# A pair search on VectorE: decoding the selected pairs on a grid, with GpSimd's weight splits held back

## The chip, the cores and the metric

The kernel is one program on one core of a Trainium2 chip. The metric is device time in microseconds (us) of one execution, as a median of several runs. A core has five engines with a queue of their own each: TensorE (PE in the rows, PEld for its weight loads), VectorE (DVE), ScalarE (ACT), GpSimd (POOL) and SyncE (SP), which here only issues transfers. An engine works its queue in order; engines wait for each other by semaphores.

## The reference, cut to what matters

Two transformer blocks on 512 tokens of width 1024. The change lies in the expert layer (PEER) of the first block, between a mixing layer and a second block that it does not touch:

```python
q = (hf @ w_query).reshape(t, 8, 256)            # 8 heads
s1 = einsum('thd,hnd->thn', q[..., :128], keys1) # 128 keys each
s2 = einsum('thd,hnd->thn', q[..., 128:], keys2)
v1, i1 = top_k(s1, 16);  v2, i2 = top_k(s2, 16)
cand = (v1[..., :, None] + v2[..., None, :]).reshape(t, 8, 256)
sc, ci = top_k(cand, 16)                         # the 16 best pairs
e1 = take_along_axis(i1, ci // 16);  e2 = take_along_axis(i2, ci % 16)
idx = e1 * 128 + e2                              # one of 16384 experts
gates = softmax(sc)
a = gelu(einsum('td,thkd->thk', h, peer_u[idx]))
out = einsum('thk,thkd->td', gates * a, peer_v[idx])
```

So for each token and head the kernel must know, for 16 pairs, the two key numbers e1 and e2 and the pair's score.

## The kernel before, in words

All of it is in `peer`. Tokens lie on the 128 partitions, in four tiles of 128. Three tiles (384 tokens) are computed densely: every expert's `gelu(h . u)` for all of them, times a gate matrix that is zero where an expert was not selected, times `peer_v`. The fourth tile gathers its selected rows one by one with indirect transfers.

**Key search.** `head(h)` multiplies by one chunk of `w_query` (two tiles of 24 matmuls with 512 columns each), then by the keys (`ps_s`), and ScalarE copies the scores out (`s`). VectorE does the rest: `stage1` finds the 16 best of 128 for each half (MAX8, MATCH_REPLACE8 and FIND_INDEX8, 20 instructions for each half over four token tiles), `pairs` adds the 50 pair sums that can be among the 16 best (`cand`) while GpSimd adds the 50 expert numbers that go with them (`ce`), `stage2` finds the 16 best of 50, and `onehot` (once for each token tile) compares the 16 positions with 0 to 49 (`ob`), multiplies by `ce` (`oh`) and reduces, which gives the expert number (`Ef`).

**Weights.** Each fp32 weight tile is used as a rounded part `whi` (ScalarE) and a remainder `wlo = w - whi`. Line 94 computes `wlo`, in this part of the program on GpSimd (`eng=nc.gpsimd`). Of the three matmuls for one slice of weights the third reads `wlo`. Two raw tiles and four split tiles are buffered.

**Expert groups.** `u_group(g)` multiplies 256 experts' `peer_ut` by the 384 dense tokens: two tiles of 24 matmuls with 384 columns; ScalarE applies the gelu (`ga`). 64 groups are needed. Groups 0 to 9 run behind the eight heads, 10 to 15 in the gate stage, the other 48 in the value stage (`AHEAD = 32` tiles are computed before that).

**Gate stage.** `prep` turns the expert numbers and gates over (`ps_tr`). 96 calls of `g_build`, for four tokens each: VectorE compares with the two key numbers (`o1`, `o2`), GpSimd multiplies `o2` by the gate, TensorE multiplies the two (`ps_g`), ScalarE copies to `stg`; after eight calls 2 MB go to DRAM (`gd`). 

**Value stage.** For each tile of 128 experts the gates come back from DRAM (`gq`), multiply `ga`, and 18 matmuls add to six accumulators (`acc`); `u_group` is called every second tile, and the gathered rows are worked on beside it.

`todo` and `pull` say where the pieces of work are written; the framework's scheduler then sets the order within each engine's queue from what each piece needs, so written order is only a wish.

Of the kernel before, what the change touches and what calls it, by code (L numbers as in the profile page):

```python
# [8 lines left out]
F32 = mybir.dt.float32  # L9
F32R = mybir.dt.float32r  # L10
BF16 = mybir.dt.bfloat16
I32 = mybir.dt.int32
# [13 lines left out]
TT = T // P  # L26
AHEAD = 32
U1 = 10
# [23 lines left out]
class Kernel:  # L52
    def __init__(self, ctx, tc, io, tap=None):
        self.ctx, self.tc, self.nc, self.io = ctx, tc, tc.nc, io
        self.tap = tap or (lambda name, ap: None)
        self.sqtag = ("sq", "sqsum", 1, self.nc.vector)
        nc = self.nc
        self.const = ctx.enter_context(tc.tile_pool(name="const", bufs=1))
        self.res = ctx.enter_context(tc.tile_pool(name="res", bufs=1))
        self.wraw = ctx.enter_context(tc.tile_pool(name="wraw", bufs=2))  # L60
        self.wsp = ctx.enter_context(tc.tile_pool(name="wsp", bufs=4))
        self.act = ctx.enter_context(tc.tile_pool(name="act", bufs=1))
        self.tmp = ctx.enter_context(tc.tile_pool(name="tmp", bufs=2))
# [423 lines left out]
    def peer(self, x, r):  # L487
# [7 lines left out]
        nc.gpsimd.iota(it, pattern=[[1, P]], base=0, channel_multiplier=0, allow_small_or_imprecise_dtypes=True)  # L495
        Ef = c.tile([P, TT, 8, 16], F32, name="Ef")
        gt = c.tile([P, TT, 8, 16], F32, name="gt")
# [7 lines left out]
        with ExitStack() as st:  # L505
# [12 lines left out]
            with ExitStack() as s2:  # L518
                sp = s2.enter_context(tc.tile_pool(name="p_sel", bufs=2))
                pp = s2.enter_context(tc.tile_pool(name="p_ps", bufs=1, space=PSUM))  # L520
                it16 = sp.tile([P, 50, 16], BF16, bufs=1, name="it16")
                nc.vector.tensor_copy(it16, it[:, 0:50].unsqueeze(2).to_broadcast([P, 50, 16]))
                keys = sp.tile([P, 8, 2, P], F32, bufs=1, name="keys")
# [9 lines left out]
                def head(h):  # L533
# [29 lines left out]
                    box = {}  # L563

                    def pairs():
                        cand = sp.tile([P, TT, 50], F32, tag="cand", name="cand")
                        ce = sp.tile([P, TT, 50], F32, tag="ce", name="ce")
                        fi = sp.tile([P, 2, TT, 16], F32, tag="fi", name="fi")
                        nc.gpsimd.tensor_scalar(fi[:, 0], ix[:, :, 0, :], 128.0, None, op0=ALU.mult)
                        nc.gpsimd.tensor_copy(fi[:, 1], ix[:, :, 1, :])  # L570
                        o = 0
                        for i in range(8):
                            n = 16 // (i + 1)
                            nc.vector.tensor_tensor(cand[:, :, o:o + n], v[:, :, 0, i:i + 1].to_broadcast([P, TT, n]),
                                                    v[:, :, 1, 0:n], op=ALU.add)
                            nc.gpsimd.tensor_tensor(ce[:, :, o:o + n], fi[:, 0, :, i:i + 1].to_broadcast([P, TT, n]),
                                                    fi[:, 1, :, 0:n], op=ALU.add)
                            o += n
                        nc.vector.tensor_tensor(cand[:, :, o:50], v[:, :, 0, 8:16],
                                                v[:, :, 1, 0:1].to_broadcast([P, TT, 8]), op=ALU.add)  # L580
                        nc.gpsimd.tensor_tensor(ce[:, :, o:50], fi[:, 0, :, 8:16],
                                                fi[:, 1, :, 0:1].to_broadcast([P, TT, 8]), op=ALU.add)
                        box["cand"], box["ce"] = cand, ce

                    def stage2():
                        cand = box["cand"]
                        c2 = sp.tile([P, TT, 50], F32, tag="c2", name="c2")
                        sv = sp.tile([P, TT, 16], F32, tag="sv", name="sv")
# [10 lines left out]
                        for t in range(TT):  # L599
                            nc.vector.max_index(px[:, t, 8:16], sv[:, t, 8:16], c2[:, t, :])  # L600
                        pf = sp.tile([P, TT, 16], BF16, tag="pf", name="pf")
                        nc.vector.tensor_copy(pf, px)
                        box["pf"] = pf
# [3 lines left out]
                    def onehot(t):  # L607
                        ob = sp.tile([P, 50, 16], BF16, tag="ob", bufs=2, name="ob")
                        nc.vector.tensor_tensor(ob, it16, box["pf"][:, t, :].unsqueeze(1).to_broadcast([P, 50, 16]),
                                                op=ALU.is_equal)  # L610
                        oh = sp.tile([P, 16, 50], F32, tag="oh", bufs=2, name="oh")
                        nc.vector.tensor_tensor(oh, ob.rearrange("p c k -> p k c"),
                                                box["ce"][:, t, :].unsqueeze(1).to_broadcast([P, 16, 50]),
                                                op=ALU.mult)
                        nc.vector.tensor_reduce(Ef[:, t, h, :], oh, AX.X, ALU.add)

                    todo.extend([lambda: stage1(0), lambda: stage1(1), pairs, stage2] +
                                [lambda t=t: onehot(t) for t in range(TT)])

                for h in range(8):  # L620
                    head(h)
                    pull(4)
                for g in range(U1):
                    u_group(g, nc.gpsimd)
                    pull(3)
                pull(len(todo))
                g3 = gt.rearrange("p t h k -> p (t h) k")
# [8 lines left out]

            ah.append(st.enter_context(tc.tile_pool(name="p_ah1", bufs=AHEAD - 2 * U1)))
            Ei = c.tile([P, TT, P], I32, name="Ei")
            GQ = 32
            gd = st.enter_context(tc.tile_pool(name="p_dram", bufs=1, space=bass.MemoryType.DRAM)).tile(  # L640
                [NG // GQ, P, P, GQ], F32, name="gd")
            with ExitStack() as s3:
# [6 lines left out]
                def prep():  # L649
                    nc.vector.tensor_copy(Ei, Ef.rearrange("p t h k -> p t (h k)"))  # L650
                    scr = sp.tile([P, 3, 3, P], F32, tag="stg", name="scr")
                    e1, e1i, e2 = scr[:, 0], scr[:, 1].bitcast(I32), scr[:, 2]
                    nc.vector.tensor_scalar(e1i, Ei[:, 0:3, :], 7, None, op0=ALU.arith_shift_right)
                    nc.vector.tensor_copy(e1, e1i)
                    nc.vector.scalar_tensor_tensor(e2, e1, -128.0, Ef[:, 0:3].rearrange("p t h k -> p t (h k)"),
                                                   op0=ALU.mult, op1=ALU.add)
                    for i, src in enumerate((e1, e2, gt[:, 0:3].rearrange("p t h k -> p t (h k)"))):
                        ps = pp.tile([P, 4, P], F32, tag="g", name="ps_tr")
# [26 lines left out]
                for g in range(U1, AHEAD // 2):  # L685
                    pull(16)
                    u_group(g, nc.gpsimd)
                pull(len(todo))

            with ExitStack() as s4:  # L690
# [12 lines left out]
                def issue(n):  # L703
                    if n >= 2 * P:
# [6 lines left out]
                        out=rows[n], out_offset=None, in_=io[src],  # L711
                        in_offset=bass.IndirectOffsetOnAxis(ap=Ei[:, 3, j:j + 1], axis=0))
                    if len(done) > PACE:
# [685 lines left out]
```

## Time and profile before

| what | us |
|---|---|
| median of 3 runs | 3067.05 (3049.09, 3067.05, 3068.01) |
| profiled execution, its own time | 3052.26 |
| its span in the trace | 3050.5 |
| TensorE busy, of the span | 2882.1 (94%) |
| VectorE busy, of the span | 2066.8 (68%) |
| GpSimd busy, of the span | 768.9 (25%) |

The whole span is mostly TensorE's, so what counts is where TensorE is not busy. A view by stretches shows that; the chain of waits and the rows of single instructions say why. Matmul records overlap (a matmul of 512 columns shows 0.39 us, but the next starts 0.23 us later), so a stretch is costed by the distance between starts.

### The profile page before, as it was taken

What the parts mean: (1) busy time and instruction counts of PE and PEld (TensorE: products, weight loads), DVE (VectorE), ACT (ScalarE), POOL (GpSimd) and SP (SyncE); (2) the same over time, 40 slices, a digit from 0 to 9 for tenths busy, and PEclk for the clock granted to TensorE, in tenths of its full rate; (3) what the DMA queues carried; (4) which work ended last, traced back from release to release, by engine and by line L of the source; (5) the groups of instructions that cost most, each with busy time, mean ns of one, the idle gap of its engine ahead of it and who ended that gap; (6) DMA issues with size and microseconds to landing.
All of it is one profiled execution on the core that took longest, in us unless ns stands there. A gap on an engine that the chain in (4) does not pass through costs nothing. (4 is left out here: it accounts for less than half of the span.)

```text
span 3050.5 us, 39516 instructions
## 1 busy us (share of the span) xinstructions
PE 2882.1 (94%) x14965; PEld 2460.7 (81%) x14965; DVE 2066.8 (68%) x3945; ACT 1222.2 (40%) x2014; POOL 768.9 (25%) x646
## 2 busy tenths in 40 slices
PE   7989678879999999999998999999999999999998
PEld 5777677867999999989986777888887888878886
DVE  7979998767877787777876445444546776654453
ACT  6543125743333333333335435333335554443223
POOL 0013447743555554554431000000011010000000
PEclk9999798989999999999999999999999999999999
DMA  7541223578888888878862222222222011132221
GB/s 263 172 175 56 68 78 146 203 249 291 317 286 301 287 308 290 292 279 293 300 249 76 66 81 70 97 97 97 97 70 74 24 56 35 31 115 97 97 97 56
DMA packets 131937, 483.03 MB, mean 158 GB/s; under 512 B 10017, under 2 KB 59425, under 8 KB 95778
## 3 DMA queue, kind: packets, MB, share of 16 engines
q1 hardware_dynamic: 94016, 345.13, 32.4%
q0 software_dynamic: 36864, 134.23, 12.0%
q8 instruction: 118, 1.93, 0.3%
q10 hardware_dynamic: 866, 1.13, 0.1%
q14 instruction: 73, 0.60, 0.1%
HBM read 453.20 MB, written 27.26 MB: 158 GB/s over the span
## 5 line engine op out<-in xcount | busy, mean ns | idle before, releaser
L93 ACT ACTIVATE whi<-wraw 128x1024 fp32r<-128x1024 f32 (+2 forms) x500 | 522.5, 1046 | 1053.9 <-PE lin L122 708.2
L121 PE MATMUL lin<-xah,whi 128*128 128x512 f32 (+1 forms) x2144 | 798.4, 373 | 30.1 <-ACT ga L514 19.8
L123 PE MATMUL lin<-xah,wlo 128*128 128x512 f32 (+1 forms) x2144 | 794.2, 371 | 4.7 <-POOL wlo L94 4.7
L122 PE MATMUL lin<-xal,whi 128*128 128x512 f32 (+1 forms) x2144 | 794.2, 371 | 2.8 <-DVE xal L810 2.8
L94 DVE TENSOR_TENSOR wlo<-wraw,whi 128x1024 fp32r<-128x1024 f32 (+2 forms) x388 | 481.8, 1242 | 178.9 <-ACT whi L93 178.6
L94 POOL TENSOR_TENSOR wlo<-wraw,whi 128x1024 fp32r<-128x1024 f32 x112 | 298.3, 2673 | 779.1 <-ACT whi L93 682.6
L121 PEld LDWEIGHTS lin<-xah,whi 128*128 128x128 f32 x2144 | 407.1, 190 | 82.4 <-ACT ga L514 20.8
L122 PEld LDWEIGHTS lin<-xal,whi 128*128 128x128 f32 x2144 | 407.7, 190 | 49.5 <-DVE xal L810 5.1
L123 PEld LDWEIGHTS lin<-xah,wlo 128*128 128x128 f32 x2144 | 407.4, 190 | 49.3 <-POOL wlo L94 5.3
L721 DVE SCALAR_TENSOR_TENSOR gacc<-rows,acol,gacc 128x1024 f32<-128x1024 f32 x128 | 185.2, 1447 | 106.9 <-DMA rows<-peer_v,Ei 106.5
L769 PE MATMUL acc<-whi,gah 128*128 128x512 f32 x768 | 238.9, 392 | 19.5 <-ACT gah L93 19.5
L723 DVE CUSTOM_DVE_ANT_0 rows<-rows,hrow 128x1024 f32<-128x1024 f32 x128 | 191.1, 1493 | 96.9 <-DMA rows<-peer_u,Ei 96.7
L769 PE MATMUL acc<-whi,gal 128*128 128x512 f32 x768 | 239.5, 393 | 7.9 <-DVE gal L94 7.9
L769 PE MATMUL acc<-wlo,gah 128*128 128x512 f32 x768 | 238.1, 391 | 0.8 <-DVE wlo L94 0.8
L710 POOL DMA_INDIRECT rows<-peer_u,Ei x128 | 161.0, 1258 | 196.0 <-PE acc L769 143.0
L122 PE MATMUL lin<-hl,whi 128*128 128x512 f32 x512 | 200.1, 391 | 0.0
L121 PE MATMUL lin<-hh,whi 128*128 128x512 f32 x512 | 199.3, 389 | 0.0
L123 PE MATMUL lin<-hh,wlo 128*128 128x512 f32 x512 | 199.2, 389 | 0.0
L710 POOL DMA_INDIRECT rows<-peer_v,Ei x128 | 153.4, 1198 | 153.3 <-PE acc L769 112.0
L769 PEld LDWEIGHTS acc<-whi,gah 128*128 128x128 f32 x768 | 144.3, 189 | 47.1 <-ACT gah L93 19.8
L769 PEld LDWEIGHTS acc<-whi,gal 128*128 128x128 f32 x768 | 144.0, 189 | 41.7 <-DVE gal L94 11.6
L769 PEld LDWEIGHTS acc<-wlo,gah 128*128 128x128 f32 x768 | 144.7, 189 | 32.6 <-DVE wlo L94 1.4
(437 smaller groups left out, 4232.7 us busy)
## 6 DMA issues: line engine op xcount, KB each, us to landing
wraw<-peer_ut SPq DMA_DIRECT2D x64, 1024.0 KB, 5.2
wraw<-peer_v SPq DMA_DIRECT2D x64, 1024.0 KB, 6.3
wraw<-w_up SPq DMA_DIRECT2D x32, 1024.0 KB, 5.0
wraw<-w_down SPq DMA_DIRECT2D x32, 1024.0 KB, 5.0
gd<-stg SPq DMA_DIRECT2D x12, 2048.0 KB, 6.9
gq<-gd SPq DMA_DIRECT2D x32, 768.0 KB, 12.1
ada_w<-w_ada SPq DMA_DIRECT2D x20, 1024.0 KB, 5.2
wraw<-dn_w_in SPq DMA_DIRECT2D x16, 1024.0 KB, 5.1
```

What stands on the lines that cost most here:

```text
L93: self.nc.scalar.activation(hi, x, AF.Copy)
L94: (eng or self.nc.vector).tensor_tensor(lo, x, hi.bitcast(F32), op=ALU.subtract)
L121: nc.tensor.matmul(ps[:, :n], hi[:, i], xh[:, k, :n], start=(i == 0), stop=False)
L122: nc.tensor.matmul(ps[:, :n], hi[:, i], xl[:, k, :n], start=False, stop=False)
L123: nc.tensor.matmul(ps[:, :n], lo[:, i], xh[:, k, :n], start=False, stop=(k == ks[1] - 1))
L710: dma = nc.gpsimd.indirect_dma_start(out=rows[n], out_offset=None, in_=io[src], in_offset=bass.IndirectOffsetOnAxis(ap=Ei[:, 3, j:j + 1], ...
L721: nc.vector.scalar_tensor_tensor(gacc, t, w, gacc, op0=ALU.mult, op1=ALU.add)
L723: nc.vector.tensor_tensor_reduce(t, t, hrow, 1.0, 0.0, op0=ALU.mult, op1=ALU.add, accum_out=w)
L769: mm = nc.tensor.matmul(acc[t][d], w[:, ts], r[:, d * T:(d + 1) * T], start=(e == 0 and f == 0), stop=(e == P - 1 and f == 2))
```

## The change

Four parts.

1. **Grid and decoding.** The pair sums are laid out as a grid: 80 places in place of 50, written by three instructions in place of nine. The position in the grid gives row and column by shifts and comparisons; one comparison of 2048 bf16 elements with 0 to 15, one product with the key numbers and four halving sums then give e1 and e2 (bf16) for all four token tiles at once. GpSimd's `ce` is gone, and `prep` need no longer take expert numbers apart.
2. **Hold.** While head h (from 2 on) and group h-1 are split, each `wlo` on GpSimd also waits for head h-2's last decoding sum.
3. **Order.** Expert groups 0 to 6 are written between the heads. One group less (`AHEAD = 30`) runs before the value stage, which then has 49.
4. **Gate stage.** `o1` and `o2` have four buffers, not three; the twelfth gate write goes out in four pieces.

```diff
-AHEAD = 32
+AHEAD = 30
     def split(self, hi, lo, x, eng=None):
         self.nc.scalar.activation(hi, x, AF.Copy)
-        (eng or self.nc.vector).tensor_tensor(lo, x, hi.bitcast(F32), op=ALU.subtract)
+        ins = (eng or self.nc.vector).tensor_tensor(lo, x, hi.bitcast(F32), op=ALU.subtract)
+        if eng is not None and self.hold is not None:
+            self.after(ins, self.hold)
...
+                    C = 80
                     def pairs():
...
+                        nc.vector.tensor_tensor(cand[:, :, 16:72].rearrange("p t (i j) -> p t i j", j=8),
+                                                v0[:, :, 1:8].unsqueeze(3).to_broadcast([P, TT, 7, 8]),
+                                                v1[:, :, 0:8].unsqueeze(2).to_broadcast([P, TT, 7, 8]), op=ALU.add)
...
+                    def decode():
+                        px, sv = box["px"].bitcast(I32), box["sv"]
...
+                        nc.vector.tensor_scalar(rc[:, 0], px, 3, None, op0=ALU.arith_shift_right)
+                        nc.vector.tensor_scalar(rc[:, 1], px, 7, None, op0=ALU.bitwise_and)
...
+                        nc.vector.tensor_copy(ib, ix)
+                        oh = sp.tile([P, TT * 2 * 16, 16], BF16, tag="oh", bufs=1, name="oh")
+                        nc.vector.tensor_tensor(oh, it16, ij.rearrange("p t u k -> p (t u k)").unsqueeze(2)
+                                                .to_broadcast([P, P, 16]), op=ALU.is_equal)
+                        o4 = oh.rearrange("p (g k) i -> p g k i", k=16)
+                        nc.vector.tensor_tensor(o4, o4, ib.rearrange("p t u i -> p (t u) i").unsqueeze(2)
+                                                .to_broadcast([P, 2 * TT, 16, 16]), op=ALU.mult)
+                        for n in (8, 4, 2):
+                            nc.vector.tensor_tensor(oh[:, :, 0:n], oh[:, :, 0:n], oh[:, :, n:2 * n], op=ALU.add)
...
+                        return nc.vector.tensor_tensor(e, o5[:, :, :, 0], o5[:, :, :, 1], op=ALU.add)
...
+                last = []
                 for h in range(8):
-                    head(h)
-                    pull(4)
...
+                    self.hold = last[-2] if h > 1 else None
+                    last.append(head(h))
+                    if h:
+                        u_group(h - 1, nc.gpsimd)
+                self.hold = None
+                for g in range(7, U1):
                     u_group(g, nc.gpsimd)
...
-                    o1 = sp.tile([P, 4, P], F32, tag="o1", bufs=3, name="o1")
-                    o2 = sp.tile([P, 4, P], F32, tag="o2", bufs=3, name="o2")
+                    o1 = sp.tile([P, 4, P], F32, tag="o1", bufs=4, name="o1")
+                    o2 = sp.tile([P, 4, P], F32, tag="o2", bufs=4, name="o2")
...
-                        nc.sync.dma_start(out=gd[t0 // GQ], in_=box["stg"])
+                        cuts = (0, 8, 32, 64, P) if t0 + 4 == NG else (0, P)
+                        for a, b in zip(cuts, cuts[1:]):
+                            nc.sync.dma_start(out=gd[t0 // GQ][:, a:b, :], in_=box["stg"][:, a:b, :])
```

What this makes of three queues (line numbers of the changed kernel are 1 to 27 higher). GpSimd in the key search, before, at the first heads:

```order
L94 TENSOR_TENSOR wlo<-wraw,whi 128x1024 x2
L569 TENSOR_SCALAR fi<-ix 128x64
L94 TENSOR_TENSOR wlo<-wraw,whi 128x1024
L570 CAST fi<-ix 128x64
L576 TENSOR_TENSOR ce<-fi 128x4x16
L576 TENSOR_TENSOR ce<-fi 128x4x8
```

and with the change, from the first head to the gate stage (`o` is `o2`):

```order
L95 TENSOR_TENSOR wlo<-wraw,whi 128x1024 x4
L498 IOTA iota 128x128
L95 TENSOR_TENSOR wlo<-wraw,whi 128x1024 x36
L694 TENSOR_TENSOR o_3968<-o_3968,tr 128x512
```

The pair numbers are gone: GpSimd has nothing but splits until the gates begin. There, six single splits stand among the 96 products, where eight stood before.

VectorE at the end of head 0, before (one half of the four token tiles):

```order
L604 TENSOR_TENSOR gt<-sv 128x4x16
L602 CAST pf<-px 128x64
L609 TENSOR_TENSOR ob<-it_1871,pf 128x800 x2
L612 TENSOR_TENSOR oh<-ob,ce 128x800 x2
L615 TENSOR_REDUCE Ef<-oh 128x16 x2
```

and with the change (L555 is already head 1's first MAX8, L557 its MATCH_REPLACE8):

```order
L555 MAX v<-s 128x8
L620 TENSOR_TENSOR oh<-it_1871,ij 128x2048
L555 MAX v<-s 128x8
L623 TENSOR_TENSOR oh<-oh,ib 128x2048
L555 MAX v<-s 128x8
L626 TENSOR_TENSOR oh<-oh 128x128x8
L557 MATCH_REPLACE s_2161<-v,s 128x128
L626 TENSOR_TENSOR oh<-oh 128x128x4
L557 MATCH_REPLACE s_2161<-v,s 128x128
L626 TENSOR_TENSOR oh<-oh 128x128x2
L557 MATCH_REPLACE s_2161<-v,s 128x128
L631 TENSOR_TENSOR Ef<-oh 128x4x32
```

The next head's first searches now stand ahead of this head's last sum (L631), the one that GpSimd is held on two heads later.

ScalarE where the softmax's exponential stands, before (`ga` is an expert group's gelu):

```order
L514 ACTIVATE ga<-lin 128x384
L629 ACT_TABLE_LOAD
L629 ACTIVATE gt<-gt 128x512
L93 ACTIVATE whi<-wraw 128x1024
L514 ACT_TABLE_LOAD
L514 ACTIVATE ga<-lin 128x384
```

and with the change (`scr` are the copies of e1 and e2 in `prep`):

```order
L517 ACTIVATE ga<-lin 128x384
L650 ACT_TABLE_LOAD
L650 ACTIVATE gt<-gt 128x512
L517 ACT_TABLE_LOAD
L517 ACTIVATE ga<-lin 128x384
L94 ACTIVATE whi<-wraw 128x1024 x2
L517 ACTIVATE ga<-lin 128x384
L673 ACTIVATE scr<-Ef 128x384 x2
```

Ahead of the exponential stand the gelus of groups 0 to 6 now, and behind it those of 7, 8 and 9.

## Rows read from the trace of the kernel before

**Rows 1.** Windows: length, busy us per engine (instructions), granted clock, DMA share, GB/s.

```profile
236.00:481.00 245.00, 187.70 (x934) 170.35 (x933) 244.67 (x959) 61.95 (x87) 109.70 (x122) 0.88 0.22 74
481.00:642.00 161.00, 143.01 (x1065) 138.93 (x1063) 124.43 (x196) 116.87 (x123) 121.85 (x105) 0.98 0.46 185
...
775.00:1595.00 820.00, 817.56 (x4121) 741.63 (x4120) 631.54 (x688) 290.24 (x403) 406.55 (x267) 1.00 0.81 290
```

**Rows 2.** The same view, two stretches of 25 us inside the key search.

```profile
250.00:275.00 25.00, 25.00 (x127) 20.85 (x125) 24.96 (x97) 7.86 (x12) 7.33 (x14) 1.00 0.25 80
...
325.00:350.00 25.00, 15.17 (x63) 13.09 (x64) 25.00 (x111) 5.49 (x8) 9.98 (x14) 0.69 0.13 43
```

**Rows 3.** Timeline, VectorE, search: start, duration, work; last the final head.

```profile
235.85 0.87 DVE L552 MAX8 v<-s 128x8 f32<-128x128 f32 x4 [5.31 <-ACT s L547]
...
245.22 1.07 DVE L574 TENSOR_TENSOR cand<-v 128x64 f32<-128x64 f32 x8
...
246.42 0.55 DVE L591 MAX8 sv<-cand 128x8 f32<-128x50 f32 x4
...
249.50 0.82 DVE L604 TENSOR_TENSOR gt<-sv 128x64 f32<-128x64 f32 x1
...
263.49 0.87 DVE L552 MAX8 v<-s 128x8 f32<-128x128 f32 x4
...
460.68 0.62 DVE L604 TENSOR_TENSOR gt<-sv 128x64 f32<-128x64 f32 x1
...
473.92 1.90 DVE L615 TENSOR_REDUCE Ef<-oh 128x16 f32<-128x800 f32 x2
```

**Rows 4.** Durations by line, 225 to 480 us: shortest/median/longest, first and last start.

```profile
L609 DVE TENSOR_TENSOR ob<-it,pf x32: 550/564/2614, 250.5 to 470.1; 128x800 bf16<-128x800 bf16 x32
...
L612 DVE TENSOR_TENSOR oh<-ob,ce x32: 1573/1727/3865, 251.4 to 472.3; 128x800 f32<-128x800 bf16 x32
...
L602 DVE CAST pf<-px x8: 178/2360/2404, 250.2 to 461.2; 128x64 bf16<-128x64 uint32 x8
...
L94 POOL TENSOR_TENSOR wlo<-wraw,whi x35: 2340/2398/3966, 233.6 to 476.9; 128x1024 fp32r<-128x1024 f32 x35
```

**Rows 5.** The page: VectorE's full-precision subtract (busy us, mean ns of one).

```profile
L94 DVE TENSOR_TENSOR wlo<-wraw,whi 128x1024 fp32r<-128x1024 f32 (+2 forms) x388 | 481.8, 1242 | 178.9 <-ACT whi L93 178.6
```

**Rows 6.** Timeline, TensorE: scores of two heads, expert matmuls, stall, transposes.

```profile
246.75 1.05 PE L545 MATMUL ps_s<-keys,q 128*128 128x128 f32 x8
...
259.54 1.05 PE L545 MATMUL ps_s<-keys,q 128*128 128x128 f32 x8
...
440.77 0.33 PE L122 MATMUL lin<-xal,whi 128*128 128x384 f32 x1
...
449.61 0.33 PE L122 MATMUL lin<-xal,whi 128*128 128x384 f32 x1
...
464.77 0.69 PE L121 MATMUL lin<-xah,whi 128*128 128x384 f32 x1 [14.65 <-ACT ga L514]
...
480.76 1.10 PE L660 MATMUL ps_tr<-ident,scr 128*128 128x128 f32 x6 [0.79 <-PE lin L123]
```

**Rows 7.** Timeline of TensorE late in the gate stage; then its longest wait there.

```profile
624.93 1.05 PE L676 MATMUL ps_g<-o,o 128*128 128x128 f32 x8
...
632.89 1.05 PE L676 MATMUL ps_g<-o,o 128*128 128x128 f32 x8
...
PE ps_g L676 <- POOL o L674: 17.6, 10, 2.3
```

**Rows 8.** Timeline, TensorE, end of gate stage; then a DMA row (page).

```profile
638.60 1.16 PE L676 MATMUL ps_g<-o,o 128*128 128x128 f32 x8 [0.41 <-POOL o L674]
...
641.35 0.34 PE L123 MATMUL lin<-xah,wlo 128*128 128x384 f32 x1
661.15 1.22 PE L769 MATMUL acc<-whi,gah 128*128 128x512 f32 x2 [19.45 <-ACT gah L93]
...
gd<-stg SPq DMA_DIRECT2D x12, 2048.0 KB, 6.9
```

More of the change, by code (lines that the diff above doesn't have):

```diff
@@ L571, in pairs @@
[L571 to L583, printed above, removed]
+                        cand = sp.tile([P, TT, C], F32, tag="cand", name="cand")
@@ new lines, in pairs @@
+                        v0, v1 = v[:, :, 0, :], v[:, :, 1, :]
+                        nc.vector.tensor_tensor(cand[:, :, 16:72].rearrange("p t (i j) -> p t i j", j=8),
+                                                v0[:, :, 1:8].unsqueeze(3).to_broadcast([P, TT, 7, 8]),
+                                                v1[:, :, 0:8].unsqueeze(2).to_broadcast([P, TT, 7, 8]), op=ALU.add)
+                        nc.vector.tensor_tensor(cand[:, :, 0:16], v0[:, :, 0:1].to_broadcast([P, TT, 16]), v1,
+                                                op=ALU.add)
@@ L585, in stage2 @@
+                        nc.vector.tensor_tensor(cand[:, :, 72:80], v0[:, :, 8:16],
+                                                v1[:, :, 0:1].to_broadcast([P, TT, 8]), op=ALU.add)
+                        box["cand"] = cand
                     def stage2():
                         cand = box["cand"]
-                        c2 = sp.tile([P, TT, 50], F32, tag="c2", name="c2")
+                        c2 = sp.tile([P, TT, C], F32, tag="c2", bufs=1, name="c2")
                         sv = sp.tile([P, TT, 16], F32, tag="sv", name="sv")
@@ L600, in stage2 @@
                             nc.vector.max_index(px[:, t, 8:16], sv[:, t, 8:16], c2[:, t, :])
-                        pf = sp.tile([P, TT, 16], BF16, tag="pf", name="pf")
-                        nc.vector.tensor_copy(pf, px)
-                        box["pf"] = pf
+                        box["px"], box["sv"] = px, sv
+                    def decode():
+                        px, sv = box["px"].bitcast(I32), box["sv"]
+                        rc = sp.tile([P, 2, TT, 16], I32, tag="rc", name="rc")
+                        nc.vector.tensor_scalar(rc[:, 0], px, 3, None, op0=ALU.arith_shift_right)
+                        nc.vector.tensor_scalar(rc[:, 1], px, 7, None, op0=ALU.bitwise_and)
+                        rf = sp.tile([P, 2, TT, 16], F32, tag="rf", name="rf")
+                        nc.vector.tensor_copy(rf, rc)
+                        r, q = rf[:, 0], rf[:, 1]
+                        w = sp.tile([P, 3, TT, 16], F32, tag="w", name="w")
+                        ij = sp.tile([P, TT, 2, 16], BF16, tag="ij", name="ij")
+                        m, a, b = [w[:, i] for i in range(3)]
+                        nc.vector.scalar_tensor_tensor(m, r, 9.0, q, op0=ALU.is_equal, op1=ALU.mult)
+                        nc.vector.scalar_tensor_tensor(a, r, 1.0, r, op0=ALU.is_ge, op1=ALU.subtract)
+                        nc.vector.tensor_tensor(ij[:, :, 0, :], m, a, op=ALU.subtract)
+                        nc.vector.tensor_scalar(b, r, 1.0, 8.0, op0=ALU.is_equal, op1=ALU.mult)
+                        nc.vector.tensor_tensor(b, b, q, op=ALU.add)
+                        nc.vector.tensor_tensor(ij[:, :, 1, :], b, m, op=ALU.subtract)
+                        ib = sp.tile([P, TT, 2, 16], BF16, tag="ib", name="ib")
+                        nc.vector.tensor_copy(ib, ix)
[7 more added lines that the diff above has]
+                            nc.vector.tensor_tensor(oh[:, :, 0:n], oh[:, :, 0:n], oh[:, :, n:2 * n], op=ALU.add)
+                        e = Ef[:, :, h].rearrange("p t u k -> p t (u k)")
+                        o5 = oh.rearrange("p (t g) i -> p t g i", t=TT)
@@ L617, in head @@
-                    todo.extend([lambda: stage1(0), lambda: stage1(1), pairs, stage2] +
-                                [lambda t=t: onehot(t) for t in range(TT)])
-                for h in range(8):
-                    head(h)
-                    pull(4)
-                for g in range(U1):
+                        return nc.vector.tensor_tensor(e, o5[:, :, :, 0], o5[:, :, :, 1], op=ALU.add)
+                    stage1(0)
+                    stage1(1)
+                    pairs()
+                    stage2()
@@ L624, in peer @@
+                    return decode()
+                last = []
+                for h in range(8):
+                    self.hold = last[-2] if h > 1 else None
+                    last.append(head(h))
+                    if h:
+                        u_group(h - 1, nc.gpsimd)
+                self.hold = None
+                for g in range(7, U1):
                     u_group(g, nc.gpsimd)
-                    pull(3)
-                pull(len(todo))
                 g3 = gt.rearrange("p t h k -> p (t h) k")
@@ L649, in prep @@
                 def prep():
-                    nc.vector.tensor_copy(Ei, Ef.rearrange("p t h k -> p t (h k)"))
                     scr = sp.tile([P, 3, 3, P], F32, tag="stg", name="scr")
[L652 to L657, printed above, removed]
+                    for i in range(2):
+                        nc.scalar.activation(scr[:, i].rearrange("p t (h k) -> p t h k", k=16), Ef[:, 0:3, :, i, :],
+                                             AF.Copy)
+                    nc.vector.scalar_tensor_tensor(Ei.rearrange("p (h k) -> p h k", k=16), Ef[:, 3, :, 0, :], 128.0,
+                                                   Ef[:, 3, :, 1, :], op0=ALU.mult, op1=ALU.add)
+                    for i, src in enumerate((scr[:, 0], scr[:, 1], gt[:, 0:3].rearrange("p t h k -> p t (h k)"))):
                         ps = pp.tile([P, 4, P], F32, tag="g", name="ps_tr")
```

30 lines of the change are left out of this document (9 added, 21 removed).

## The prediction, made before the changed kernel ran

> **What bounds the kernel now.** I read the view by stretches first, to see where TensorE, 94% busy over the whole span, is not. From 775 us on it is full: 817.56 of 820 us at clock 1.00 [rows 1], so nothing is to be had there, and what is moved there is paid in full. In the key search it is busy 187.70 of 245 us, and VectorE 244.67 [rows 1]: that stretch is VectorE's. In the gate stage TensorE is busy 143.01 of 161 us, and VectorE, ScalarE and GpSimd 117 to 124 each [rows 1]: four engines in lock step, none full. The clock follows: with TensorE busy 25.00 of 25 us it was granted 1.00 (2.4 GHz), with 15.17 of 25 us 0.69, a mixture with 1.2 GHz [rows 2].
>
> Next the timeline of VectorE, from the search's first MAX8 at 235.85 to its last reduce, which ends at 475.82 [rows 3]: 240.0 us for 8 heads, **30.0 us a head**. In head 0 the two searches of 128 take 9.37 us (to 245.22), the pair sums 1.20, the search of 50 takes 3.08 (to 249.50), and the other 14 us go to `gt`, `pf` and `onehot`.
>
> Then durations by line. `pf`, a cast of 64 elements, takes 178 ns at best and 2360 at the median; `ob` 550 at best and 2614 at worst; `oh` 1573 and 3865 [rows 4]. The excess is always near 2.1 to 2.3 us, and a split `wlo` on GpSimd lasts 2398 ns [rows 4]: these instructions wait for one to end.
>
> **The change, part by part.** *VectorE's work for a head.* The searches stay: 9.37. Three grid sums in place of nine: 0.7. The search of 80 lies between that of 50 (3.08) and half the searches of 128 (9.37/2 = 4.69, as many instructions): 3.08 + 30/78 x 1.61 = 3.7. `gt` 0.2. Ten small instructions of decoding at the 178 ns of `pf` alone: 1.8. The comparison of 2048 bf16 elements has no row. At `ob`'s best rate (550 ns for 800) it is 1.4 us; at the 1242 ns for 1024 of a full-precision subtract [rows 5] 2.5; at `oh`'s strided rate (1573 for 800) 4.0. I take 2.4: like `ob` its operands are bf16, but one of them repeats a single element 16 times, so I don't count on `ob`'s rate. The product, 2048 in contiguous runs, at `ob`'s rate: 1.4. Three halving sums of 1024, 512 and 256: 0.7, 0.4 and 0.25. The last sum reads 128 elements with a stride, as `oh` does: 0.3. Together **21.2 us** (20.2 to 23.5).
>
> *The hold.* Once head h-2's last sum is in, GpSimd splits four tiles, 4 x 2.4 = 9.6 us; meanwhile VectorE searches head h-1, which takes 9.37 us and reads one tensor an instruction. So the splits should be over when the decoding, which suffers from them, comes. They end about when the grid sums begin; for a part of one split there I add 0.7: 21.9 us.
>
> The Trainium skill, page SBUF — State Buffer, section Who interferes with whom, speaks against the change: a VectorE instruction with two SBUF inputs and a GpSimd instruction that reads SBUF exclude each other for a whole instruction, and the decoding has many two-input instructions. The excess in `ob` and `oh` agrees [rows 4]. By the page alone, with splits and decoding falling together as before, nothing would be won here; the hold is what decides, and rival 2 is that case.
>
> *TensorE's cycle.* From one head's scores to the next 12.79 us pass [rows 6]: projection and scores. A group adds 48 matmuls at 8.84/51 = 0.1733 us [rows 6], 8.32. Together 21.1 us, just under VectorE's 21.9. A cycle c of 21.9 with TensorE near full should keep the full clock.
>
> *Does the hold delay it?* From release: split 2.4, projection 48 matmuls 10.9, copies and scores 2.5, then the rest of the previous head's decoding, which stands behind the new head's first MAX8 on VectorE, 2.3. That is 18.1 us, within 21.9: no wait.
>
> *End of the search.* Head 0 ends at 235.85 + 21.2 = 257.1, head 6 at 257.1 + 6c. Head 7's `gt` follows 13.2 later (searches, less four MAX8 already done, grid, search of 80). The exponential on ScalarE waits for it, and groups 8 and 9 on TensorE wait behind: the same wait shows before as 14.65 us up to 464.77, 3.5 us after `gt` (460.68 + 0.62) [rows 3, 6]. Groups 8 and 9 then take 16.6, and 2.2 for the clock after the stall. So the transposes start at 293 + 6c = **425** where they started at 480.76 [rows 6]: **-56 us**. With c at TensorE's 21.1 it is 420 (-61); with one whole split more in each head, c = 23.6, it is 435 (-46).
>
> *Gate stage.* Six builds took 7.96 us with 15 group matmuls among them [rows 7]: 5.36 without, 0.894 for a build. Before: 96 builds 85.8, 288 matmuls 49.9, transposes 1.2, together 136.9; it took 160.8 (480.76 to 641.5). So 23.9 us were lost, the largest wait TensorE's on GpSimd's product, 17.6 us in 10 waits [rows 7]; eight splits stood among the products, 3.0 us for each. Now one group less runs here (-8.3, which leaves 128.6), six splits stand there, and the fourth buffer lets VectorE run one build (1.3 us) further ahead: 6 x 1.7 = 10 us lost. That makes 139, **-22 us** (-32 if nothing is lost, -14 if the buffer does nothing).
>
> *Value stage.* The group that moved costs 8.3 us where TensorE is full: **+8.3**.
>
> *The last gate write.* TensorE stood still for 19.45 us from the last gates to the first value matmul [rows 8]. Before, 11 group matmuls (2 us) filled its start; now none is left, +2. The write takes 6.9 us [rows 8]; in pieces the first gates are in DRAM earlier, but `gq` stands behind all four pieces on SyncE's queue and reads the same rows of DRAM: at most 6 us gained, at least nothing. I take 1, so **+1** (-4 to +2). The other edits (a wider table of 0 to 15, ScalarE's copies in `prep`) lie in waits: VectorE idles 5.31 us ahead of the first MAX8 [rows 3].
>
> **Sum:** -56 - 22 + 8.3 + 1 = -69 on the profiled execution's 3052.3: 2984. It stands 14.8 below the median of the runs (3049 to 3068); I add half of that: **2990**.
>
> **The rivals.** *1. The gate stage stays in lock step* (18%): the splits cost what they did and the buffer nothing, so that only the moved group leaves: -8.3 in place of -22, about 3005. For it: GpSimd's products and splits alone are 121.85 us of the stage's 161 [rows 1], and ScalarE's copies 117.
>
> *2. The hold doesn't part splits and decoding* (7%). Four splits in 22 us can catch more two-input instructions than before; if a head stays near 30 us, the search ends at 473, 8 us earlier, and the total is 3052 - 8 - 22 + 9 + 7 = 3038: no difference. Against it: the splits need 9.6 us and the searches give 9.4 free of them.
>
> *3. The hold starves TensorE and the clock falls* (5%, slower). If the release of a split comes late, TensorE idles in each cycle, is granted 1.2 GHz as at 325 us [rows 2], and its 21.1 us become 42. The search then ends at 293 + 253 = 546, 65 later: 3052 + 65 - 13 + 7 = 3111. It decides from c = 33: there the gains behind the search are used up. Against it: 21.1 of 21.9 us is as full as the stretch with clock 1.00.
>
> **How the numbers follow.** The forecast has 70%. Its bounds are -61 - 32 + 8.3 - 4 = -89, and -46 - 14 + 8.3 + 2 = -50 with the median's full 14.8 added: 2963 to 3017. Rival 1 falls in it; rivals 2 and 3 lie outside. The range is 2960 to 3018. What a measurement can tell from no change is 1%, here 31 us: faster means under 3036. The forecast, rival 1 and a little of rival 2 make 90% faster; the rest of rival 2 is 5% same; rival 3 is 5% slower.
>
> **What would show it.** VectorE's MAX8 of successive heads 21 to 23 us apart, and the comparison near 2.4 us; the product at most 1.5 us with no long outliers in heads 1 to 5; the clock at 1.00 all through the search; the transposes near 425; 139 us from there to the last gates; about 19 to 21 us of stillness behind it. Heads 25 us or more apart would make the prediction wrong, and so would a clock under 0.9 there, or a value stage longer by more than one group.

## The result and the profile after

Median 3009.38 us (3007.77 to 3015.08, 4 runs) against 3065.31 (3049.09 to 3068.01, 4 runs): ratio **0.9834** [0.9814, 0.9853], faster by 1.7%. Forecast were 2990, range 2960 to 3018. The profiled execution took 3015.08 us, its span 3013.4.

The medians are 56 us apart, the two profiled executions 37: the one before (3052.26) lies low among its kernel's times, the one after is the longest of its four. The stretches below compare these two executions; in which stretch the other 19 us lie no trace here shows.

Three stretches first. The view of the changed kernel's stretches gives their bounds, then the length, busy time and count of TensorE, its weight loads, VectorE, ScalarE and GpSimd, then granted clock, DMA share and GB/s. The bounds are 236 us as in [rows 1] (the first MAX8 stands at 237.16), the transposes, the last build's end; and the value matmuls from first to last. Behind them, the last two stretches of the kernel before.

```profile
236.00:429.01 193.01, 179.58 (x940) 162.49 (x939) 179.29 (x932) 63.48 (x90) 83.21 (x35) 0.96 0.27 93
429.01:583.74 154.73, 140.15 (x1018) 137.54 (x1016) 124.14 (x195) 113.98 (x120) 116.20 (x103) 0.93 0.44 178
608.64:1564.36 955.72, 941.85 (x4656) 843.56 (x4656) 726.96 (x818) 331.55 (x459) 452.71 (x301) 1.00 0.80 286
...
480.76:639.76 159.00, 141.32 (x1055) 137.56 (x1056) 124.67 (x196) 115.60 (x122) 121.85 (x105) 0.98 0.46 186
661.15:1601.16 940.01, 931.32 (x4608) 834.29 (x4608) 720.91 (x818) 328.67 (x455) 445.80 (x299) 1.00 0.81 290
```

The transposes start at 429.0 where they started at 480.8 [rows 6]: **-51.8**. From there to the first value matmul 179.6 us pass, 180.4 before (480.76 to 661.15 [rows 6, 8]): **-0.8**. The value stage takes 955.7 us for 4656 matmuls; the kernel before took 940.0 for 4608: **+15.7**. Together -36.9, and the spans differ by 37.1.

In the middle of the search TensorE is full now, where [rows 2] show 15.17 us of 25 at clock 0.69; over the whole search the clock is 0.96.

```profile
325.00:350.00 25.00, 24.95 (x133) 22.41 (x132) 24.69 (x143) 8.49 (x12) 13.06 (x6) 1.00 0.24 85
```

VectorE's decoding in the search, all heads together; columns are minimum, median and maximum in ns, first and last start in us.

```profile
L626 DVE TENSOR_TENSOR oh<-oh x24: 408/452/2941, 256.5 to 417.2; 128x1024 bf16<-128x1024 bf16 x8, 128x512 bf16<-128x512 bf16 x8, 128x256 bf16<-128x256 bf16 x8
L620 DVE TENSOR_TENSOR oh<-it,ij x8: 2274/2292/2293, 252.8 to 407.9; 128x2048 bf16<-128x2048 bf16 x8
L623 DVE TENSOR_TENSOR oh<-oh,ib x8: 1204/1226/2800, 255.2 to 410.7; 128x2048 bf16<-128x2048 bf16 x8
L631 DVE TENSOR_TENSOR Ef<-oh x8: 399/426/448, 258.6 to 417.7; 128x128 bf16<-128x128 bf16 x8
```

The comparison (L620) takes 2.29 us in every head, the product 1.23 at the median. Compare the medians with the maxima: a split still falls into the decoding now and then. The timeline of VectorE and GpSimd shows where it doesn't (head 3 to head 4) and where it does (head 6); columns are start, duration, engine, line.

```profile
323.31 0.44 DVE L631 TENSOR_TENSOR Ef<-oh 128x128 bf16<-128x128 bf16 x1
323.99 9.49 POOL L95 TENSOR_TENSOR wlo<-wraw,whi 128x1024 fp32r<-128x1024 f32 x4 [11.93 <-DVE v L555]
333.03 0.70 DVE L573 TENSOR_TENSOR cand<-v 128x224 f32<-128x224 f32 x1
...
381.76 2.37 POOL L95 TENSOR_TENSOR wlo<-wraw,whi 128x1024 fp32r<-128x1024 f32 x1 [1.51 <-ACT whi L94]
381.79 2.42 DVE L615 TENSOR_TENSOR w<-w,rf 128x64 f32<-128x64 f32 x1
...
388.08 2.41 POOL L95 TENSOR_TENSOR wlo<-wraw,whi 128x1024 fp32r<-128x1024 f32 x1 [3.95 <-ACT whi L94]
388.09 3.91 DVE L626 TENSOR_TENSOR oh<-oh 128x1024 bf16<-128x1024 bf16 x3
```

Four splits run right behind the last sum, while VectorE searches, and end as the grid sums begin. The splits of groups 7 to 9 have no hold in the program, and two of them fall into head 6's decoding: an add of 64 elements takes 2.42 us beside a split of 2.37. Last sums of successive heads are 21.4 to 21.8 us apart up to head 5 and 25.9 and 25.7 in heads 6 and 7.

TensorE's timeline at the end of the search; the bracket is its idle time ahead and what ended it.

```profile
408.83 0.69 PE L124 MATMUL lin<-xah,whi 128*128 128x384 f32 x1 [9.32 <-ACT ga L517]
420.55 0.44 PE L124 MATMUL lin<-xah,whi 128*128 128x384 f32 x1 [1.21 <-ACT ga L517]
429.01 0.82 PE L680 MATMUL ps_tr<-ident,scr 128*128 128x128 f32 x6
```

This answers to the 14.65 us of [rows 6]. The gate stage, GpSimd's splits and TensorE's waits there:

```profile
439.39 2.37 POOL L95 TENSOR_TENSOR wlo<-wraw,whi 128x1024 fp32r<-128x1024 f32 x1 [1.19 <-ACT whi L94]
...
442.81 1.29 PE L696 MATMUL ps_g<-o,o 128*128 128x128 f32 x8 [2.32 <-POOL o L694]
...
456.83 2.37 POOL L95 TENSOR_TENSOR wlo<-wraw,whi 128x1024 fp32r<-128x1024 f32 x1 [2.19 <-ACT whi L94]
...
460.25 1.64 PE L696 MATMUL ps_g<-o,o 128*128 128x128 f32 x8 [2.29 <-POOL o L694]
...
477.52 1.82 PE L696 MATMUL ps_g<-o,o 128*128 128x128 f32 x8 [2.29 <-POOL o L694]
```

Six splits stand among the products, some 17.3 us apart. GpSimd waits for ScalarE's copy (1.19 us at the first split, 2.2 at the others) and splits for 2.37, and TensorE stands for 2.3; the eight matmuls behind take 1.29, then 1.64, then 1.82. The stage's clock is 0.93; before it was 0.98. Behind the gates:

```profile
593.25 1.08 SPq L777 DMA_DIRECT2D gq<-gd  x2
594.38 3.19 SPq L101 DMA_DIRECT2D wraw<-peer_v  x1
607.35 1.49 DVE L784 TENSOR_TENSOR ga<-ga,gq 128x384 f32<-128x384 f32 x3
608.64 1.22 PE L793 MATMUL acc<-whi,gah 128*128 128x512 f32 x2 [24.90 <-ACT gah L94]
```

TensorE stands for 24.90 us where it stood 19.45 [rows 8]: `gq` is issued 9.5 us behind the last gates and used 14.1 us later; before, 8.4 and 11.8.

### The profile page after: what moved, and what is told of

Read it like the earlier page. It is cut to its first block, busy times and chain, and to the rows that moved or that the text cites. A ratio compares the mean times of both kernels' runs of the same rounds, so it can differ in the third digit from the quotient of the medians.

```text
span 3013.4 us, 39409 instructions
## 1 busy us (share of the span) xinstructions
PE 2883.6 (96%) x14965; PEld 2462.2 (82%) x14965; DVE 2011.0 (67%) x3918; ACT 1223.4 (41%) x2016; POOL 740.5 (25%) x558
## 5 line engine op out<-in xcount | busy, mean ns | idle before, releaser
L95 DVE TENSOR_TENSOR wlo<-wraw,whi 128x1024 fp32r<-128x1024 f32 (+2 forms) x388 | 488.2, 1260 | 175.9 <-ACT whi L94 175.7
L95 POOL TENSOR_TENSOR wlo<-wraw,whi 128x1024 fp32r<-128x1024 f32 x112 | 291.3, 2615 | 855.4 <-ACT whi L94 682.9
L793 PE MATMUL acc<-whi,gah 128*128 128x512 f32 x768 | 238.4, 392 | 24.9 <-ACT gah L94 24.9
L734 POOL DMA_INDIRECT rows<-peer_v,Ei x128 | 159.8, 1249 | 162.6 <-PE acc L793 127.3
```

Of the source, the lines that this page charges most:

```text
L95: ins = (eng or self.nc.vector).tensor_tensor(lo, x, hi.bitcast(F32), op=ALU.subtract)
L734: dma = nc.gpsimd.indirect_dma_start(out=rows[n], out_offset=None, in_=io[src], in_offset=bass.IndirectOffsetOnAxis(ap=Ei[:, j:j + 1], axi ...
L793: mm = nc.tensor.matmul(acc[t][d], w[:, ts], r[:, d * T:(d + 1) * T], start=(e == 0 and f == 0), stop=(e == P - 1 and f == 2))
```

## The experiments

All times below are of each run's profiled execution, but for the ratios. "Gate stage" is from the transposes to the last build's end, "gap" from there to the first value matmul; "behind" counts group matmuls in the gap.

| kernel | transposes | gate stage | gap | behind | value stage | median us | ratio to before |
|---|---|---|---|---|---|---|---|
| before | 480.8 | 159.0 | 21.4 | 11 | 940.0 | | |
| changed | 429.0 | 154.7 | 24.9 | 0 | 955.7 | 3009.4 | 0.9834 [0.9814, 0.9853] |
| no hold | 444.2 | 154.9 | 25.0 | 0 | 953.6 | 3029.4 | 0.9909 [0.9881, 0.9936] |
| decoding alone | 456.5 | 160.4 | 22.9 | 43 | 946.8 | 3032.5 | 0.9910 [0.9885, 0.9934] |
| three buffers | 425.7 | 156.3 | 24.5 | 0 | 952.5 | 3010.0 | 0.9851 [0.9817, 0.9885] |
| one piece | 427.3 | 151.7 | 24.7 | 0 | 960.0 | 3014.4 | 0.9858 [0.9833, 0.9883] |
| VectorE splits | 429.9 | 128.6 | 32.0 | 140 | 952.2 | 2992.4 | 0.9781 [0.9752, 0.9810] |
| VectorE splits, groups among builds | 429.5 | 138.0 | 22.8 | 0 | 951.0 | 2992.2 | 0.9786 [0.9762, 0.9811] |
| last groups behind | 429.3 | 128.0 | 24.6 | 132 | 949.2 | 2985.7 | 0.9764 [0.9740, 0.9788] |
| exponential later | 421.8 | 154.6 | 25.2 | 0 | 955.6 | 3004.4 | 0.9822 [0.9794, 0.9850] |
| both edits | 422.4 | 129.6 | 23.7 | 132 | 951.9 | 2980.3 | 0.9744 [0.9718, 0.9769] |
| both, 32 tiles ahead | 419.1 | 140.9 | 24.6 | 132 | 941.3 | 2975.3 | 0.9719 [0.9699, 0.9739] |

**No hold.**

```diff
-                    self.hold = last[-2] if h > 1 else None
+                    self.hold = None
```

> The changed kernel without the hold: GpSimd's splits of a group start as soon as ScalarE's copies are there. Theory (the hold parts splits and decoding): the splits fall into the decoding, the products, halving sums and grid sums of heads 2 to 7 each meet one now and then and last 2 to 3 us longer, a head goes from 21.9 to 24 to 28 us, and the transposes start at 440 to 465 us in place of 429; total 3020 to 3045. Rival (the decoding has so few long two-input instructions that splits don't matter to it): long outliers of the product no more frequent, transposes at 425 to 433, total as with the hold, 3005 to 3015.

The theory held: transposes at 444.2, 15.2 later; heads 24.6 to 27.4 us apart but for head 6 (21.0). The summary of the product over all heads, and the timeline of head 2:

```profile
L623 DVE TENSOR_TENSOR oh<-oh,ib x8: 1225/3260/3309, 251.0 to 425.9; 128x2048 bf16<-128x2048 bf16 x8
```

```profile
301.85 2.29 DVE L620 TENSOR_TENSOR oh<-it,ij 128x2048 bf16<-128x2048 bf16 x1
303.05 3.35 POOL L95 TENSOR_TENSOR wlo<-wraw,whi 128x1024 fp32r<-128x1024 f32 x1 [3.02 <-ACT whi L94]
304.18 3.30 DVE L623 TENSOR_TENSOR oh<-oh,ib 128x2048 bf16<-128x2048 bf16 x1
```

The product's median is 3260 ns in place of 1226. The split that began inside the comparison lasts 3.35 us, 2.3 of them after the comparison's end; the product behind takes 3.30, its own 1.23 and 2.1 of waiting. Whoever comes second waits for the rest of the other's instruction. The Trainium skill, page SBUF — State Buffer, section Who interferes with whom, states such an exclusive lock between a VectorE instruction with two SBUF inputs and a GpSimd instruction that reads SBUF; these rows agree, in both directions.

**The decoding alone.**

```diff
-                    self.hold = last[-2] if h > 1 else None
+                    self.hold = None
...
-                    if h:
-                        u_group(h - 1, nc.gpsimd)
...
-                for g in range(7, U1):
+                for g in range(U1):
```

with three buffers, one piece and `AHEAD = 32` as before; where the groups stand among the builds is still as in the changed kernel.

> The grid decoding alone: no hold, all heads ahead of groups 0 to 9 in the program, three buffers, the last write in one piece, 32 tiles ahead. Theory (the search is VectorE's, 21.9 us a head against 30.0 before; hold and order of groups only keep the splits out of the decoding): if TensorE's order interleaves groups with heads, heads 23 to 26 us apart and the transposes at 435 to 455; if the ten groups fall behind the search, heads near 21 and then up to 83 us of groups, transposes at 460 to 490. Value stage 940 as before in either case (no group moved into it), total 3000 to 3050.

Transposes at 456.5, 24.3 earlier than before, just past the first case. The last sum ends at 429.1, so VectorE's part is done 46.7 us before 475.8 [rows 3], but TensorE is behind. The view by stretches shows it idle in the middle of the search, with the clock down:

```profile
300.00:325.00 25.00, 19.24 (x88) 16.20 (x87) 25.00 (x128) 5.50 (x8) 7.07 (x3) 0.87 0.17 50
325.00:350.00 25.00, 19.53 (x90) 17.44 (x89) 25.00 (x124) 5.01 (x7) 4.68 (x2) 0.86 0.21 78
350.00:375.00 25.00, 14.36 (x69) 14.04 (x68) 25.00 (x120) 5.74 (x9) 8.07 (x3) 0.73 0.13 43
```

So of the search's -51.8 the decoding alone gives 24.3, a group behind each head 12.3 more (no hold: 444.2), and the hold 15.2. These shares are good to some 5 us, since the searches do not begin at the same time (first MAX8 at 235.9 before, 237.9, 232.4 and 237.2 in this order); counted from there they are 26.3, 6.8 and 20.0.

**Three buffers.**

```diff
-                    o1 = sp.tile([P, 4, P], F32, tag="o1", bufs=4, name="o1")
-                    o2 = sp.tile([P, 4, P], F32, tag="o2", bufs=4, name="o2")
+                    o1 = sp.tile([P, 4, P], F32, tag="o1", bufs=3, name="o1")
+                    o2 = sp.tile([P, 4, P], F32, tag="o2", bufs=3, name="o2")
```

> The changed kernel with three buffers for the gate comparisons in place of four. As predicted (a buffer lets VectorE run one build of 1.3 us further ahead of each of six splits): the gate stage 7 to 9 us longer, 161 to 163 in place of 154, total 3015 to 3020. Rival (a split costs the same 3.9 us with either number, since VectorE is not ahead when it comes): 153 to 156 us, total 3005 to 3012.

Gate stage 156.3, 1.6 us longer, not 7 to 9. Kernels that are alike in this stage differ by more (151.7 with one piece, 154.9 with no hold), and from the first split to the sixth 86.5 us pass with four buffers and 86.7 with three: between the splits the buffer is worth nothing. The rows show where its lead goes; first the changed kernel at its split of 456.83 (above), then the same split with three buffers.

```profile
454.81 1.08 ACT L698 ACTIVATE stg<-ps_g 128x512 f32<-128x512 f32 x1 [0.32 <-PE ps_g L696]
455.68 1.07 ACT L94 ACTIVATE whi<-wraw 128x1024 fp32r<-128x1024 f32 x1
461.93 0.69 DVE L692 TENSOR_TENSOR o<-itp,tr 128x512 f32<-128x512 f32 x1 [3.34 <-PE ps_g L696]
...
453.52 2.38 POOL L95 TENSOR_TENSOR wlo<-wraw,whi 128x1024 fp32r<-128x1024 f32 x1 [0.96 <-ACT whi L94]
456.95 1.16 PE L696 MATMUL ps_g<-o,o 128*128 128x128 f32 x8 [2.31 <-POOL o L694]
```

With four buffers VectorE has four builds ready when the split ends (three with three), and stands for 3.34 us until TensorE frees a buffer. But GpSimd, further ahead too, waits 2.19 us for the copy `whi` ahead of the split in place of 0.96: in ScalarE's queue `whi` stands behind the copy of an earlier build (`stg`). TensorE stands 2.3 us either way. The total cannot be told from the changed kernel's.

**Splits of the gate stage on VectorE.**

```diff
-                    u_group(g, nc.gpsimd)
+                    u_group(g)
```

> The changed kernel with the splits of the groups of the gate stage (the last five) on VectorE in place of GpSimd. Theory 1 (each split on GpSimd holds up the products behind it, 2.4 us and the wait for ScalarE's copy ahead of it, some 3.9 us on TensorE): from the transposes to the last gates 132 to 143 us in place of 154, total 2990 to 3000. Rival (four engines in lock step, whatever the split's engine: what GpSimd is rid of VectorE is given, and the waits go with it): 150 to 160 us, total 3005 to 3015.

128.6 us, less than the 132 to 143 of the theory. But the run changed two things: the order on TensorE came out otherwise, with 140 group matmuls behind the last gates. Two runs separate them.

**The same, with the groups kept among the builds.**

```diff
-                    if g < AHEAD // 2 - 3:
-                        pull(24)
-                    else:
-                        pull(len(todo))
-                    u_group(g, nc.gpsimd)
+                    pull(16)
+                    u_group(g)
+                pull(len(todo))
```

> The changed kernel with the splits of the gate stage's groups on VectorE, and these groups among the builds as in the changed kernel (222 group matmuls between the first gates and the last, none behind). If the engine counts: VectorE, the fullest engine of the stage at some 1.30 us a build, takes ten splits of 1.22: 96 x 1.30 + 12 + 4 = 141 us in place of 154.7, then 25 us of stillness as before; first value matmul near 596, total 2996 to 3002. If the place counts: 150 to 155 us and 25; first value matmul at 605 to 610, total 3005 to 3012.

The engine counts: 138.0 us with as many matmuls in the stage as in the changed kernel (x1018), at clock 1.00, by the view by stretches:

```profile
429.50:567.53 138.03, 134.77 (x1018) 130.20 (x1016) 131.85 (x203) 113.02 (x120) 104.01 (x96) 1.00 0.50 200
```

That is 16.7 us less; TensorE and VectorE are both nearly full.

**GpSimd's splits of the last three groups held behind the builds.**

```diff
+                    box.setdefault("mm", []).append(mm)
...
                         pull(len(todo))
+                        self.hold = box["mm"][-3]
                     u_group(g, nc.gpsimd)
+                self.hold = None
```

> The changed kernel with GpSimd's splits of the last three groups made to wait for the last build's matmul, so that 132 group matmuls stand behind the last gates, as 140 do in the run with VectorE's splits; the splits stay on GpSimd. If the engine of the splits was what counted there (3.9 us each among the products; four are left among them here): the gate stage 140 to 148 us in place of 154.7, then some 32 us of groups in place of the 24.9 of stillness; first value matmul at 602 to 610, total 3003 to 3012. If the place of the groups was what counted: gate stage about 130, then 32; first value matmul near 591, total 2990 to 2997.

2985.7 us, a little below the second case. My premise for the first did not come true: I had expected four splits left among the products, but those of groups 10 and 11 were over by 433 us, and none stood among the products until the last two builds. So the run does not speak against the engine; it shows the stage without splits. Its stretches, the timeline at the last builds, and the first value matmul:

```profile
429.25:557.21 127.96, 121.47 (x887) 109.90 (x886) 116.70 (x192) 108.39 (x108) 108.02 (x100) 1.00 0.47 192
581.84:1531.05 949.21, 938.13 (x4656) 839.79 (x4656) 726.78 (x824) 333.70 (x463) 457.50 (x301) 1.00 0.81 291
```

```profile
550.30 4.70 POOL L95 TENSOR_TENSOR wlo<-wraw,whi 128x1024 fp32r<-128x1024 f32 x2 [0.15 <-ACT stg L699]
...
556.05 1.16 PE L696 MATMUL ps_g<-o,o 128*128 128x128 f32 x8 [1.67 <-POOL o L694]
...
581.84 0.50 PE L796 MATMUL acc<-whi,gah 128*128 128x512 f32 x1 [1.72 <-ACT gah L94]
```

The builds go at VectorE's pace (25.00 us of 25 busy from 500 to 525 us and again to 550, 1.2 us a build), and the gap is as long as in the changed kernel (24.6 us) but filled: TensorE stands 1.72 us ahead of the value stage. Against 154.7, the six splits and the matmuls among the builds had cost 26.7 us.

What a split costs by itself is seen in stretches of ten builds with some 25 group matmuls each: with a split in the changed kernel, with a split in the kernel with one piece (below), where the clock stayed up, and behind the last split of the changed kernel.

```profile
456.83:474.10 17.27, 14.97 (x105) 14.65 (x105) 12.63 (x21) 11.79 (x13) 12.61 (x11) 0.90 0.48 184
...
453.50:469.10 15.60, 13.31 (x105) 12.99 (x104) 12.48 (x21) 11.74 (x13) 12.49 (x11) 1.00 0.53 204
...
549.08:562.35 13.27, 13.27 (x107) 13.27 (x106) 12.77 (x21) 11.84 (x13) 10.52 (x11) 1.00 0.47 196
```

A split costs 2.3 us, the time that TensorE stands, and 1.7 more where the clock falls behind it: 4.0 us in the changed kernel, where it fell behind each of the six. In the stretch without a split TensorE is full (13.27 of 13.27 us); only where the group matmuls are gone too, as above, does VectorE give the pace.

**One piece.**

```diff
-                        cuts = (0, 8, 32, 64, P) if t0 + 4 == NG else (0, P)
+                        cuts = (0, P)
```

> The changed kernel with its last gate write in one piece. As predicted (pieces give 1 us): the stillness between the last gates and the first value matmul 24 to 27 us in place of 24.9, total 3006 to 3014. Rival (the four issues on SyncE's queue ahead of the gates' read, and four transfers in place of one, cost more than they give): 21 to 23 us, total 3004 to 3008. Second rival (the first gates in DRAM early are what lets the read start): 27 to 31 us.

The gap is 24.7 us, and the read of the gates waits as it did in four pieces:

```profile
588.28 1.18 SPq L777 DMA_DIRECT2D gq<-gd  x2
602.43 1.49 DVE L784 TENSOR_TENSOR ga<-ga,gq 128x384 f32<-128x384 f32 x3
```

9.3 us from the last gates to `gq`, 14.1 from there to its use: the pieces change neither. The totals overlap within their intervals. The gate stage, the same program up to its last write, took 3.0 us less, since the clock stayed at 1.00 behind the first two splits.

**The exponential later.**

```diff
-                    nc.scalar.activation(A[e], ps[:, :NG], AF.Gelu)
+                    self.gel[e] = nc.scalar.activation(A[e], ps[:, :NG], AF.Gelu)
...
-                nc.scalar.activation(g3, g3, AF.Exp)
+                self.after(nc.scalar.activation(g3, g3, AF.Exp), self.gel[17])
```

> The changed kernel with the softmax exponential made to wait on ScalarE for the gelu of tile 17, so that the gelus and copies of groups 7 and 8 are not behind it. Theory (TensorE's stalls of 9.3 and 1.2 us ahead of the transposes are those gelus behind the exponential, which waits for the last head's gt): both stalls go, and the transposes start at 417 to 422 us in place of 429, total 2997 to 3003. Rival (TensorE is ahead of VectorE there; the transposes need the last head's decoding anyway, whose last sum ends some 8 us behind gt): the stall moves behind the groups, transposes at 425 to 430, total 3005 to 3012.

TensorE's timeline at the transposes:

```profile
421.77 1.54 PE L681 MATMUL ps_tr<-ident,scr 128*128 128x128 f32 x6 [5.29 <-ACT scr L674]
```

7.2 us earlier; the two stalls of 9.32 and 1.21 us are gone, and one of 5.29 stands in their place, for the last head's decoding. Both theories held in part. The median, 5 us lower, agrees in sign, but the intervals overlap.

**Both edits, and both with 32 tiles ahead.** The two diffs above; the second also has

```diff
-AHEAD = 30
+AHEAD = 32
```

and three buffers.

> The changed kernel with the last three groups behind the gates (as in the run with their splits held) and the softmax exponential behind the gelu of tile 17. The two edits meet in different stretches, so they should add: transposes at 421 to 423 in place of 429, gate stage 127 to 130, first value matmul 573 to 577, value stage 948 to 951; total 2976 to 2982, faster than both kernels. If the 7 us before the transposes only turn up as a later wait: 2983 to 2988.

They add: 422.4, 129.6, 2980.3 us.

> The same two edits with 32 tiles ahead and three buffers: one more group of 48 matmuls (8.3 us of TensorE) leaves the value stage and joins the builds. If the builds are VectorE's at 1.30 us (96 of them 125 us, against 86 + 24 = 110 us of TensorE), the group is hidden there but for its two splits and the missing buffer (0 to 5 us): gate stage 128 to 134, value stage 940 to 943, total 2969 to 2978. If TensorE is too full for it again, as where all five groups lay among the builds: gate stage 138 to 150, total 2980 to 2992.

2975.3 us, the fastest here, 1.2% under the changed kernel by the ratios. Both cases hold in part: the group leaves the value stage (941.3, 10.6 less), but the gate stage takes 140.9, 11.3 more. That TensorE is too full for the group is not what the trace shows: two splits stand among the products again, and TensorE waits for both.

```profile
434.21 2.08 PE L697 MATMUL ps_g<-o,o 128*128 128x128 f32 x8 [2.31 <-POOL o L695]
451.64 1.16 PE L697 MATMUL ps_g<-o,o 128*128 128x128 f32 x8 [2.30 <-POOL o L695]
```

The first twenty products take 33.9 us in place of 26.1, 7.8 of the 11.3. The intervals of the two overlap, so between them nothing is decided.

## Why the prediction came out as it did

**The sum: in the range, in part by luck.** On the profiled execution -69 was forecast, with bounds of -89 and -50; -37 came. Of the 32 us that are missing 13 don't show in the median: the forecast had added 7 us for the spread of the runs, and the changed kernel's profiled execution lies 6 above its own median. Two of the prediction's own signs of being wrong showed, too: heads 6 and 7 came more than 25 us apart, and the value stage grew by nearly two groups.

**The search: right in its mechanism, -51.8 against -56.** 21.5 us a head up to head 5 (21.9 forecast), the comparison 2.29 (2.4), TensorE full. The hold decided less than the prediction says: without it the search still won 36.6 us, where rival 2 gave 8. What was off is head 6, 25.9 in place of 21.9, where splits without a hold met the decoding. From the last head's `gt` (406.3) to the transposes passed 22.7 us, 22.3 forecast. Rival 2 needed heads near 30, rival 3 a starved TensorE; the first is what no hold comes nearer to (25), the second what the decoding alone shows in part (clock 0.73).

**The gate stage: the step that failed.** By its own terms -22 was forecast and -6.1 came (160.8 to 154.7): rival 1, with 18%. What failed is the price of a split, 1.7 us: the 3.0 read from the rows before, less 1.3 because "the fourth buffer lets VectorE run one build (1.3 us) further ahead". A split cost 4.0. The buffer's build was made, but GpSimd waited it out in front of ScalarE's copy, and TensorE stood 2.3 us at a split as with three buffers. And the clock, 0.98 in this stage before, was 0.93 now: it fell behind all six splits, while before it stayed up behind most of the eight. Six splits at 4.0 on the forecast's 128.6 make 152.6, and 154.7 came. The rest of the reading was right: 128.6 without loss is near the 127 that 96 builds take at 13.27 us for ten, and the wait of TensorE on GpSimd was the cause of the loss; it went when the splits were moved behind the builds or to VectorE.

**The gap: +5.4 against +1.** Two of that is the missing group matmuls, as forecast. The gain of 1 for the pieces was nothing. The other 3.5 are `gq`, issued 1.1 us later and in use 2.4 us later after its issue. Weight loads were issued right behind it (594.38); that they are the cause was not tried.

**The value stage: +15.7 against +8.3.** The moved group is seen in the count, 48 matmuls more; with it back (4608 matmuls) the stage took 941.3, or 946.8 with the decoding alone. The remainder, 1 to 12 us in kernels with the same 4656 matmuls, is argued from the changed kernel alone: in its first 125 us 490 matmuls ran where 521 did before, and in the second slice of these, with DMA nearly full,

```profile
633.64:658.64 25.00, 21.02 (x89) 16.50 (x90) 20.95 (x35) 6.95 (x10) 4.92 (x5) 1.00 0.99 315
...
686.15:711.15 25.00, 23.96 (x96) 19.03 (x97) 23.20 (x40) 7.65 (x10) 5.80 (x5) 0.93 0.94 313
```

TensorE is busy for 21.02 us against 23.96 in the same slice before. Whether and which transfers arrive late there stays open.

## What to carry to other kernels

Where two engines exclude each other for whole instructions, the order of their work is worth as much as the work: of 52 us won in the search, 15 to 20 came from one wait put in the right place. Before a buffer is counted as slack, ask what its user waits for next: here the build that it allowed was made, and then waited for a copy in another engine's queue. And work that has no deadline (a group whose result is needed much later) belongs in the gap that a transfer leaves, not among work that four engines hand to each other.

## What the runs showed of the hardware

A VectorE add of 64 elements took 2.42 us beside a split, its neighbours 0.19 to 0.23; the price of a collision is set by the other engine's instruction, not by one's own. And short waits can show in the clock: with 2.3 us of standing at each of six splits the gate stage was granted 0.93, without splits 1.00, and eight gate matmuls took up to 1.82 us in place of 1.16. The same standing did not always do it. Before the change:

```profile
511.31 2.08 PE L676 MATMUL ps_g<-o,o 128*128 128x128 f32 x8 [2.31 <-POOL o L674]
...
528.45 1.16 PE L676 MATMUL ps_g<-o,o 128*128 128x128 f32 x8 [2.31 <-POOL o L674]
```

What makes the difference stays open.
